# A hybrid decoder layer on one core: direct terms of 19 blocks a feed-forward added by a transfer, with six smaller edits

## The chip, the core and the metric

The kernel runs on one core of a Trainium2 chip. Its engines work side by side, each through its own queue of instructions in order: TensorE (PE; its weight loads are PEld) multiplies matrices into PSUM banks, VectorE (DVE) and ScalarE (ACT) do elementwise work, GpSimd (POOL) here mostly issues transfers, SyncE (SP) issues the loads of weights. Sixteen DMA engines carry the transfers of all queues. The metric is the device time of one execution in microseconds (us); the median of the runs counts.

## The reference

One layer over 256 tokens with a model width of 2048, all in float32:

```python
h = layer_norm(DN_ALPHA * h + 0.5 * swiglu(h, ffn1_w_in, ffn1_w_out), ln1_g, ln1_b)
q, k, v, qi, ki, wi, rx, rg, gates = split_cols(h @ w_in)
...                      # rotary embedding of q, k, qi, ki
y_attn = dsa_attention(q, k, v, qi, ki, wi)
y_rnn = rglru_branch(rx, rg, conv_w, conv_b, lru_wa, lru_ba, lru_wx, lru_bx, lru_lambda)
g_attn, g_rnn = jnp.split(jax.nn.sigmoid(gates), 2, axis=-1)
merged = g_attn * (y_attn @ w_attn_branch) + g_rnn * (y_rnn @ w_rnn_branch)
h = layer_norm(DN_ALPHA * h + merged @ w_out, ln2_g, ln2_b)
h = layer_norm(DN_ALPHA * h + 0.5 * swiglu(h, ffn2_w_in, ffn2_w_out), ln3_g, ln3_b)
```

`swiglu` is `(silu(a) * b) @ w_out` with `a, b = split(h @ w_in)`; its inner width is 5632. The attention has 16 heads of 128; an indexer picks for each query its 64 best keys, the others are masked before the softmax. Weights come to some 460 MB, each read once.

## The kernel before, in words

**Precision by splitting.** Every float32 operand is split in a high and a low part in the format fp32r. ScalarE copies the high part (`wh`, line 243), VectorE subtracts it to get the low part (`wl`, line 244). A product is then three matmuls: high by high, low of the data by high of the weights, high of the data by low of the weights (lines 694, 695, 697). So each weight element costs one ScalarE and one VectorE pass before TensorE can use it.

**Pieces.** The weights are a single list of pieces in order of use, 512 KB each in the plain case (128 partitions by 1024). `Weights.unit` hands out parts of the current piece; when it moves to a new piece it issues loads up to ten pieces ahead (`load_to`, as far as load buffers are free: five plain ones `raw`, three double ones `rf`), emits the split of the piece four ahead (`split_to`), and then steps the background once (`on_piece`). So "n pieces behind" in this text counts such steps.

**Forms.** A chunk is four of the sixteen row tiles of a weight block. A plain chunk (`c`) is two pieces. A chunk in forms replaces eight half-size products with seven, at the price of sums on VectorE: `p1q3`, `p2`, `q5p7`, `q4p6` (function `operand`, lines 206, 210, 213), which multiply sums of weights with sums of the data (`sf`, `sh`, `sl`, function `left`). `block_plan` sets which chunks of a block are plain, which are in forms, and where pieces of an output product (`o`, a fill) stand between them.

**The feed-forwards.** Both run `ffn`: 22 blocks of 256 columns for a and as many for b. `layer_plans` gives the plans: blocks 0 and 1 plain; block 2 chunks 1 and 3 in forms and two fills; blocks 3 to 5 two or three chunks in forms and two fills; blocks 6 to 21 three chunks in forms and four fills, three of them at the head of the block. At the end of a block `gate` adds the forms' results (in banks `e`) and the direct terms (in banks `c`) into a buffer `z` (there is one), takes the silu and the product on ScalarE and VectorE, and some steps later transposes the result on TensorE and splits it to `g`. The transposes stand `LAG_T` = 7 steps behind. `fill` multiplies a segment's `g` with output weights; the segments are blocks 0 to 1, 2 to 5, 6 to 9 and so on. Its results go by ScalarE into `yd` and by an accumulating transfer of POOL's queue into `Y` (lines 1109, 1110).

**Order.** TensorE's, SP's and POOL's instructions stand in the order in which the program emits them. ScalarE's and VectorE's are put in order by a planner from its own estimates and priorities; `tc.high_priority()` moves instructions up, and `tc.issue_after(x)` keeps those inside behind `x`.

**Other places that the change touches.** The start (line 567 on) splits x and the first weight pieces alternately; a copy of one element into the buffer of the third part of x (line 571) makes its load, and all that follow it on SP's queue, wait for the first split. `head` is a step-by-step task for one attention head; its softmax scales and masks the scores in one VectorE instruction (line 1279) and finds the two row maxima in two more (line 1284). `OuterNorm.finish` does the last norm: for the second half of the tokens, blocks 0 and 1 of the output go through TensorE with a diagonal matrix (`by_pe`), 2 and 3 through VectorE alone.

## Time and profile before

| what | us |
|---|---|
| median of 3 runs | 2238.52 (2238.44 to 2239.13) |
| the profiled execution's own time | 2239.67 |
| its span, first to last instruction | 2237.9 |
| TensorE busy in the span | 2223.3 |
| VectorE busy | 2106.7 |
| ScalarE busy | 1429.8 |
| POOL busy | 125.0 |

The span is what the trace shows of the profiled execution; its own time lies 1.8 us above it. An engine's busy time counts instructions that do work and leaves waits out; matmuls are pipelined, so their durations overlap and a row's duration is longer than the distance to the next row. In a row of the order of time the columns are start, length, engine, line, operation, tiles written and read, shape and count; brackets hold the idle time before it and what ended it. The DMA engines are busy for 57.9% of the span with SP's queue and for 8.4% with POOL's.

### The profile page before, as it was taken

The page shows a single profiled execution, that of the slowest core. Times are in us where ns is not written, and L with a number is a line of the kernel's source. Part 1 is how long each engine was busy: PE and PEld are TensorE (multiplying, and loading weights), DVE is VectorE, ACT ScalarE, POOL GpSimd, SP SyncE. Part 2 cuts the span into 40 slices and gives each one's busy share as a digit, 9 for nine tenths or more (in the row PEclk, how much of TensorE's full clock was granted, in tenths as well). Part 3 has the DMA queues.
Part 4 walks back from the last instruction along what each step waited for, and adds up shares of the span by engine and source line. Part 5 has one row for each costly group of instructions (what it writes and reads, how often), then busy time and mean ns, then how long its engine had stood idle before and what let it go on. Part 6 is the DMA issues. An engine that isn't in the chain of part 4 may idle for free. (4 is left out here: it accounts for less than half of the span.)

```text
span 2237.9 us, 38642 instructions
## 1 busy us (share of the span) xinstructions
PE 2223.3 (99%) x14582; PEld 2056.6 (92%) x14582; DVE 2106.7 (94%) x3037; ACT 1429.8 (64%) x1995; POOL 125.0 (6%) x195
## 2 busy tenths in 40 slices
PE   9999999999999999999999999999999999999998
PEld 7999999999998898899999999998889999999997
DVE  8999999999999999899868879999999999999997
ACT  7666666666656655665567786555666666666663
POOL 0000000000001000001000002100000000000001
PEclk9999999999999999999999999999999999999999
DMA  9776666666675555648666668766677667676655
GB/s 328 240 227 232 233 214 226 236 222 236 225 241 194 187 198 177 210 132 302 199 192 194 197 189 324 266 214 205 229 228 230 237 220 239 223 243 215 219 200 188
DMA packets 126186, 498.61 MB, mean 223 GB/s; under 512 B 14608, under 2 KB 17424, under 8 KB 107312
## 3 DMA queue, kind: packets, MB, share of 16 engines
q1 hardware_dynamic: 107424, 451.98, 57.9%
q0 software_dynamic: 18576, 44.17, 8.4%
q8 instruction: 114, 1.87, 0.3%
q14 instruction: 72, 0.59, 0.1%
HBM read 464.63 MB, written 10.49 MB: 212 GB/s over the span
## 5 line engine op out<-in xcount | busy, mean ns | idle before, releaser
L243 ACT ACTIVATE wh<-raw 128x1024 fp32r<-128x1024 f32 (+1 forms) x569 | 575.0, 1028 | 288.6 <-PE mm L695 164.4
L244 DVE TENSOR_TENSOR wl<-raw,wh 128x1024 fp32r<-128x1024 f32 (+1 forms) x569 | 661.9, 1183 | 79.8 <-ACT wh L243 78.6
L243 ACT ACTIVATE wh<-rf 128x1024 fp32r<-128x1024 f32 (+1 forms) x438 | 393.5, 915 | 191.6 <-PE mm L695 103.6
L244 DVE TENSOR_TENSOR wl<-rf,wh 128x1024 fp32r<-128x1024 f32 (+1 forms) x438 | 450.9, 1042 | 7.2 <-ACT wh L243 1.5
L694 PE MATMUL mm<-wh,hs 128*128 128x512 f32 (+1 forms) x872 | 297.3, 350 | 0.0
L695 PE MATMUL mm<-wh,hs 128*128 128x512 f32 (+1 forms) x872 | 292.1, 344 | 0.0
L694 PE MATMUL mm<-wh,g 128*128 128x512 f32 x656 | 249.5, 380 | 1.9 <-DVE z L1076 1.9
L695 PE MATMUL mm<-wh,g 128*128 128x512 f32 x656 | 248.8, 379 | 0.5 <-DVE g L810 0.5
L243 ACT ACTIVATE wh<-ws 128x1024 fp32r<-128x1024 f32 x146 | 155.2, 1063 | 123.9 <-PE mm L695 71.7
L694 PE MATMUL bp<-wh,sh 128*128 128x256 f32 x876 | 213.6, 278 | 0.0
L695 PE MATMUL bp<-wh,sl 128*128 128x256 f32 x876 | 210.7, 275 | 0.0
L697 PE MATMUL mm<-wl,hs 128*128 128x512 f32 (+1 forms) x872 | 205.0, 344 | 0.0
L206 DVE TENSOR_TENSOR ws<-rf 128x1024 f32<-128x1024 f32 x146 | 178.3, 1221 | 8.8 <-DMA rf<-wab 2.8
L244 DVE TENSOR_TENSOR wl<-ws,wh 128x1024 fp32r<-128x1024 f32 x146 | 178.1, 1220 | 2.8 <-ACT wh L243 2.6
L694 PEld LDWEIGHTS mm<-wh,hs 128*128 128x128 f32 x872 | 165.8, 190 | 15.3 <-issue 1.3
L695 PEld LDWEIGHTS mm<-wh,hs 128*128 128x128 f32 x872 | 165.9, 190 | 13.6
L1404 PE MATMUL mm<-hs,wh 128*128 128x256 f32 x640 | 176.4, 276 | 0.0
L1405 PE MATMUL mm<-hs,wh 128*128 128x256 f32 x640 | 176.0, 275 | 0.0
L1406 PE MATMUL mm<-hs,wl 128*128 128x256 f32 x640 | 176.0, 275 | 0.0
L695 PEld LDWEIGHTS bp<-wh,sl 128*128 128x128 f32 x876 | 168.1, 192 | 1.2
L694 PEld LDWEIGHTS bp<-wh,sh 128*128 128x128 f32 x876 | 168.0, 192 | 1.2
L697 PE MATMUL mm<-wl,g 128*128 128x512 f32 x656 | 168.3, 379 | 0.0
(374 smaller groups left out, 4886.5 us busy)
## 6 DMA issues: line engine op xcount, KB each, us to landing
rf<-f1a SPq DMA_DIRECT2D x57, 1024.0 KB, 6.2
rf<-f2a SPq DMA_DIRECT2D x57, 1024.0 KB, 6.0
raw<-f1o SPq DMA_DIRECT2D x88, 512.0 KB, 7.8
raw<-f2o SPq DMA_DIRECT2D x88, 512.0 KB, 7.8
raw<-wB SPq DMA_DIRECT2D x80, 512.0 KB, 4.5
raw<-f2a SPq DMA_DIRECT2D x62, 512.0 KB, 3.9
raw<-f1a SPq DMA_DIRECT2D x61, 512.0 KB, 3.9
raw<-wG SPq DMA_DIRECT2D x54, 512.0 KB, 4.2
```

Source lines behind the costliest of these rows:

```text
L206: v.tensor_tensor(t, b[:, 0:4:3], b[:, 1:2].to_broadcast([P, 2, 4, P]), op=OP.add)
L243: nc.scalar.activation(hp, src, AF.Copy)
L244: self.last = nc.vector.tensor_tensor(lp, src, hp, op=OP.subtract)
L694: T.matmul(ps, xh, w[0], start=start, stop=False)
L695: T.matmul(ps, xl, w[0], start=False, stop=False)
L697: T.matmul(ps, xh, w[1], start=False, stop=stop)
L1404: T.matmul(ps, w[0], xh, start=first, stop=False)
L1405: T.matmul(ps, w[0], xl, start=False, stop=False)
L1406: T.matmul(ps, w[1], xh, start=False, stop=last)
```

## The change

In blocks 2 to 20 of each feed-forward, the direct terms in the banks `c` are no longer added by VectorE. ScalarE copies both banks into a new buffer `u` (4 KB a partition, one of it), and POOL's queue issues an accumulating transfer from `u` to `z`. The silu stands eight steps behind the block's end, after the high part of the piece split last; the product one step after that, behind the last low part; the transposes at the eleventh step. There are six `t` buffers instead of eight and 20 `sm` buffers instead of 21.

The plans are made for each layer. The first keeps two chunks in forms in block 2; the second has only chunk 1 there. In both, block 5 has three chunks in forms where it had two. The weights' layout follows.

At the start the loads of x and of the first four pieces are issued without the wait, and the one-element copy goes. In the softmax, two fused instructions take scores plus mask, times the negative scale, and a running minimum, in place of three; the exponential gets a scale of -1. In the last norm, block 0's first step of the second token half goes ahead of block 2's.

```diff
@@ -51,7 +51,7 @@
 
 U_BUFS = 53
 Z_BUFS = 1
-T_BUFS = 8
+T_BUFS = 6
 RAW_BUFS = 5
 RAWF_BUFS = 3
 WS_BUFS = 1
@@ -93,15 +93,16 @@
     return plan
 
 
-def layer_plans():
+def layer_plans(third=(1, 3)):
     plans = [block_plan((), 0)] * 2
-    plans += [block_plan((1, 3), 2, 0)] + [block_plan(THREE if n == 4 else (1, 3), 2, 0) for n in (3, 4, 5)]
+    plans += [block_plan(third, 2, 0)] + [block_plan(THREE if n > 3 else (1, 3), 2, 0) for n in (3, 4, 5)]
     plans += [block_plan(THREE, 4, 3)] * (NBK - 6)
     return plans
 
 
 FILLS = [(g, nb, 2 * p) for g, (b0, b1) in enumerate(SEGS[:-1]) for nb in range(4) for p in range(b1 - b0)]
 PLANS = layer_plans()
+PLANS2 = layer_plans((1,))
 A_ORDER = (6, 7, None, 4, 5, 0, 1, 2, 3)
 A_FAST = {b: () if b == 6 else ONE_A if b in (5, 1) else FAST_A for b in range(8)}
 GATE_FAST = ((), (), (), (3,), FAST_A, FAST_A, (), ())
@@ -112,12 +113,14 @@
 YR_FORMS = (0, 1)
 MG_FORMS = (0, 1)
 LAG_MG = (7, 3)
-assert sum(f == "o" for p in PLANS for f, _ in p) == len(FILLS)
+assert all(sum(f == "o" for p in q for f, _ in p) == len(FILLS) for q in (PLANS, PLANS2))
 
 OUT_LAST = ([(nb, k) for nb in (0, 1) for k in (0, 2, 4)] + [(nb, 6) for nb in (0, 1)]
             + [(nb, k) for nb in (2, 3) for k in (0, 2, 4, 6)])
 
 LAG_T = (7, 6)
+LAG_Z = 8
+LAG_D = 11
 LAG_LN = 4
 WIDE = (4, 3, 2)
 WARM = 10
@@ -240,7 +243,7 @@
             else:
                 parts = [tuple(x[:, q:min(n, q + step)] for x in (self.raw[k], h, l)) for q in range(0, n, step)]
             for src, hp, lp in parts:
-                nc.scalar.activation(hp, src, AF.Copy)
+                self.last_h = nc.scalar.activation(hp, src, AF.Copy)
                 self.last = nc.vector.tensor_tensor(lp, src, hp, op=OP.subtract)
             self.hl[self.split] = (h, l)
             if form in (None, FORMS[-1]):
@@ -454,7 +457,9 @@
         return r
 
     xs = []
-    W.load_to(1, load_x_fm)
+    W.load_to(3, load_x_fm)
+    for k2 in range(4, NK // 2):
+        load_x_fm(k2)
     cols = C([P, NCOLS], "cols")
     G.dma_start(cols, cols_d)
     posi = C([P, 2], "posi", I32)
@@ -567,11 +572,6 @@
     with tc.manual_schedule():
         for k2 in range(4):
             xs += split_x(k2)
-            if k2 == 0:
-                V.tensor_copy(xraw[2][:, :1], xs[0][:, 1, :1])
-                W.load_to(3, load_x_fm)
-                for j in range(4, NK // 2):
-                    load_x_fm(j)
             W.split_to(k2, (256, 512, PIECE, PIECE)[k2])
         for k2 in range(4, NK // 2):
             xs += split_x(k2)
@@ -967,8 +967,8 @@
                 T.matmul(ps, diag, y, start=False, stop=True)
                 A.activation(y, ps, AF.Copy)
 
+            first(1, 0)
             first(1, 2)
-            first(1, 0)
             by_pe(0)
             second(1, 2)
             leave(1, 0)
@@ -1058,8 +1058,8 @@
                 for t in range(2):
                     done(nb, ps, t)
 
-    def ffn(x, forms, ln):
-        def gate(c, e, g, i, lag, plain):
+    def ffn(x, forms, ln, plans):
+        def gate(c, e, g, i, lag, plain, by_dma):
 
             z = W.fast_pool.tile([P, 4 * S], F32, name=name("z"), tag="z", bufs=Z_BUFS)
             z4 = z.rearrange("p (j c) -> p j c", j=4)
@@ -1070,16 +1070,31 @@
                 V.tensor_tensor(z4[:, 1], z4[:, 0], p6, op=OP.add)
                 V.tensor_tensor(z4[:, 2], z4[:, 1], p7, op=OP.add)
                 V.tensor_tensor(b, q5[:, None, :].to_broadcast([P, 2, S]), z4[:, 1:3], op=OP.subtract)
-                for t in range(2):
-                    w = 512 if plain or t == 0 else S
-                    zt = z[:, t * 512:t * 512 + w]
-                    V.tensor_tensor(zt, zt, c[t][:, :w], op=OP.add)
-                A.activation(a, a, AF.Silu)
+                if by_dma:
+                    u = temps.tile([P, 4 * S], F32, name=name("cc"), tag="cc", bufs=1)
+                    for t in range(2):
+                        A.activation(u[:, t * 512:(t + 1) * 512], c[t], AF.Copy)
+                    G.dma_start(z, u, accum_op=OP.add)
+                    for _ in range(LAG_Z):
+                        yield
+                    with tc.issue_after(W.last_h.ins):
+                        A.activation(a, a, AF.Silu)
+                    yield
+                    with tc.issue_after(W.last.ins):
+                        V.tensor_tensor(a, a, b, op=OP.mult)
+                    lag = LAG_D - LAG_Z - 1
+                else:
+                    for t in range(2):
+                        w = 512 if plain or t == 0 else S
+                        zt = z[:, t * 512:t * 512 + w]
+                        V.tensor_tensor(zt, zt, c[t][:, :w], op=OP.add)
+                    A.activation(a, a, AF.Silu)
             else:
                 for t in range(2):
                     A.activation(z4[:, 2 * t], c[t][:, :S], AF.Silu)
                     A.activation(z4[:, 2 * t + 1], c[t][:, S:], AF.Copy)
-            V.tensor_tensor(a, a, b, op=OP.mult)
+            if not by_dma:
+                V.tensor_tensor(a, a, b, op=OP.mult)
             for _ in range(lag):
                 yield
             ps = BP()
@@ -1113,8 +1128,8 @@
             for n in range(b0, b1):
                 if 2 < n < 6:
                     MM(), MM()
-                c, e = blockF(x, forms, PLANS[n], fill)
-                task = gate(c, e, g[s], 2 * (n - b0), LAG_T[n == NBK - 1], ("c", 0) in PLANS[n])
+                c, e = blockF(x, forms, plans[n], fill)
+                task = gate(c, e, g[s], 2 * (n - b0), LAG_T[n == NBK - 1], ("c", 0) in PLANS[n], 1 < n < NBK - 1 and ("c", 0) in PLANS[n])
                 with tc.high_priority():
                     next(task)
                 bg.add("gate", task)
@@ -1276,15 +1291,16 @@
         T.matmul(ps[:, P:3 * P], q[:, P:], k, start=True, stop=True)
         yield
         s = U("s")[:, :3 * P]
-        V.scalar_tensor_tensor(s, ps[:, :3 * P], ATT_SCALE, bias, op0=OP.mult, op1=OP.add)
         nm = SM(2)
         sm = SM(2)
         part = (s[:, :P], s[:, P:])
         for t in range(2):
-            V.tensor_reduce(nm[:, t:t + 1], part[t], axis=AX, op=OP.max, negate=True)
+            a, b = t * P, (1 + 2 * t) * P
+            V.tensor_tensor_reduce(s[:, a:b], ps[:, a:b], bias[:, a:b], -ATT_SCALE, -2 * NEG, OP.add, OP.min,
+                                   nm[:, t:t + 1])
         yield
         for t in range(2):
-            A.activation(part[t], part[t], AF.Exp, bias=nm[:, t:t + 1], accum_out=sm[:, t:t + 1])
+            A.activation(part[t], part[t], AF.Exp, scale=-1.0, bias=nm[:, t:t + 1], accum_out=sm[:, t:t + 1])
         yield
         V.reciprocal(sm, sm)
         for t in range(2):
@@ -1528,7 +1544,7 @@
     mg = mg_forms = None
 
 
-    ffn(ln.hs, ln.forms, OuterNorm(ln3_g, ln3_b))
+    ffn(ln.hs, ln.forms, OuterNorm(ln3_g, ln3_b), PLANS2)
 
 
 def _layout(x, positions, ffn1_w_in, ffn1_w_out, ln1_g, ln1_b, w_in, conv_w, conv_b, lru_wa, lru_ba,
@@ -1550,8 +1566,8 @@
                 out[b][:, q * 2048:(q + 1) * 2048] = u.transpose(0, 5, 1, 2, 3, 4).reshape(P, -1)
         return out
 
-    def f_in(w):
-        fast = [sorted({k for f, k in plan if f in FORMS}) for plan in PLANS]
+    def f_in(w, plans):
+        fast = [sorted({k for f, k in plan if f in FORMS}) for plan in plans]
         return paired(w.reshape(NK, P, 2, NBK, 256).transpose(3, 1, 0, 2, 4).reshape(NBK, P, NK, 512), fast)
 
     def f_out(w):
```

More of the change, by code (lines that the diff above doesn't have):

```diff
@@ L343, in SM @@
     def SM(n, s="s", dt=F32):
-        return pool.tile([P, 32], dt, name=name(s), tag="sm", bufs=21)[:, :n]
+        return pool.tile([P, 32], dt, name=name(s), tag="sm", bufs=20)[:, :n]
     def C(shape, s, dt=F32):
@@ L376, in block_pieces, with ffn_pieces @@
                 pieces.append((chunk[k], f))
-    def ffn_pieces(fa, fo):
+    def ffn_pieces(fa, fo, plans):
         fills = iter(FILLS)
-        for n, plan in enumerate(PLANS):
+        for n, plan in enumerate(plans):
             block_pieces(fa[n], plan, fills, fo)
@@ L389, in wide @@
         wides.update(range(len(pieces) - n, len(pieces)))
-    ffn_pieces(f1a, f1o)
+    ffn_pieces(f1a, f1o, PLANS)
     wide(WIDE[0])
@@ L420, in tile_layer @@
     wide(WIDE[1])
-    ffn_pieces(f2a, f2o)
+    ffn_pieces(f2a, f2o, PLANS2)
     wide(WIDE[2])
@@ L1133, in tile_layer @@
     ln = InnerNorm("ln1_g", "ln1_b", FAST_A, lambda: bg.add("y", put_away()))
-    ffn(xs, xf, ln)
+    ffn(xs, xf, ln, PLANS)
     hs = ln.hs
@@ L1603, in _layout @@
         pos=c(positions[0].reshape(2, P).T),
-        f1a=f_in(ffn1_w_in[0]), f1o=f_out(ffn1_w_out[0]), wA=a_blocks(w[:, :4096], [A_FAST[b] for b in range(8)]),
+        f1a=f_in(ffn1_w_in[0], PLANS), f1o=f_out(ffn1_w_out[0]), wA=a_blocks(w[:, :4096], [A_FAST[b] for b in range(8)]),
         wki=c(ki.reshape(NK, P, P).transpose(1, 0, 2)).reshape(P, 2048), wB=b_blocks(w[:, 4176:9296].reshape(D, 2, RNN)[:, :, order].reshape(D, -1)),
@@ L1608, in _layout @@
         wrb=a_blocks(w_rnn_branch[0][order], YR_FAST),
-        wo=a_blocks(w_out[0], MG_FAST + ((),)), f2a=f_in(ffn2_w_in[0]), f2o=f_out(ffn2_w_out[0]), cols_d=c(cols),
+        wo=a_blocks(w_out[0], MG_FAST + ((),)), f2a=f_in(ffn2_w_in[0], PLANS2), f2o=f_out(ffn2_w_out[0]), cols_d=c(cols),
         ln1_g=c(ln1_g[0]), ln1_b=c(ln1_b[0]), ln2_g=c(ln2_g[0]), ln2_b=c(ln2_b[0]),
```

## The prediction

> **What bounds the kernel now.** I read the page first, then busy time by stretches of the span, then the order of time on TensorE around the few places where it stands still.
>
> ```profile
> span 2237.9 us, 38642 instructions
> PE 2223.3 (99%) x14582; PEld 2056.6 (92%) x14582; DVE 2106.7 (94%) x3037; ACT 1429.8 (64%) x1995; POOL 125.0 (6%) x195
> ```
>
> TensorE is busy for 2223.3 of 2237.9 us, so at most some 15 us of the span are not its own work. VectorE, which the change mainly relieves, is second at 94%. Busy time by stretches (columns: length, then PE, PEld, DVE, ACT, POOL, then granted clock, DMA share, GB/s):
>
> ```profile
> 0.00:6.00 6.00, 4.08 (x11) 3.27 (x12) 2.38 (x7) 2.96 (x7) 2.26 (x24) 1.00 0.63 187
> 6.00:20.00 14.00, 11.60 (x52) 9.22 (x51) 9.99 (x22) 9.67 (x22) 0.00 (x0) 1.00 1.01 374
> ...
> 1585.00:1640.00 55.00, 52.60 (x301) 46.93 (x300) 53.14 (x78) 30.21 (x42) 1.80 (x2) 1.00 0.75 247
> ...
> 1735.00:2195.00 460.00, 460.00 (x3076) 429.89 (x3075) 455.40 (x535) 299.49 (x366) 26.27 (x30) 1.00 0.67 226
> 2195.00:2238.00 43.00, 36.97 (x190) 31.17 (x188) 31.44 (x51) 12.55 (x19) 6.83 (x7) 1.00 0.46 160
> ...
> 840.00:1010.00 170.00, 169.27 (x988) 151.54 (x987) 154.47 (x343) 106.47 (x189) 5.42 (x10) 1.00 0.55 177
> ```
>
> From 1735 to 2195, fifteen like blocks of the second feed-forward, TensorE has no idle time (460.00 of 460.00), although VectorE is full too (455.40). The attention stretch is alike (169.27 of 170.00). What can be won by unloading VectorE lies only in 6 to 20 (2.4 us idle), 1585 to 1640 (2.4 us idle) and the tail (6 us). A steady block, on TensorE:
>
> ```profile
> 1735.00 0.38 PE L694 MATMUL mm<-wh,g 128*128 128x512 f32 x1
> 1742.77 0.38 PE L694 MATMUL mm<-wh,hs 128*128 128x512 f32 x1
> ...
> 1745.36 0.27 PE L694 MATMUL bp<-wh,hs 128*128 128x256 f32 x1
> ...
> 1746.70 0.28 PE L694 MATMUL mm<-wh,hs 128*128 128x256 f32 x1
> ...
> 1747.37 0.60 PE L1088 MATMUL bp<-ident,z 128*128 128x128 f32 x4
> 1747.72 0.36 PE L694 MATMUL bp<-wh,sh 128*128 128x256 f32 x1
> ...
> 1777.41 0.60 PE L1088 MATMUL bp<-ident,z 128*128 128x128 f32 x4
> ```
>
> From 1735.00 to 1742.77 three pieces of an output fill run: 7.77/3 = 2.59 us a plain piece. From 1745.36 to 1746.70 is one form of 1024 columns (1.34 us), from there to 1747.37 the half-size form p2 (0.67 us); then the four transposes of the block before hold TensorE 0.35 us. The next block's transposes come at 1777.41: a period of 30.04 us, in which TensorE never waits.
>
> **The change part by part.** Profiled time is 2239.67 us, 1.8 above its span and 1.15 above the median of 2238.52; I sum differences and set them on the median.
>
> *The transfer.* In each of 19 blocks a layer VectorE's two additions of the direct terms go, and ScalarE copies both banks out instead. The rows of the block before and of the nearest copy and transfer:
>
> ```profile
> 1739.67 0.68 DVE L1072 TENSOR_TENSOR z<-bp,z 128x512 f32<-128x512 f32 x1
> 1740.39 1.28 DVE L1076 TENSOR_TENSOR z<-z,mm 128x512 f32<-128x512 f32 x2
> ...
> 1749.29 0.42 DVE L810 TENSOR_TENSOR g<-bp,g 128x256 fp32r<-128x256 f32 x1
> ...
> 1751.36 0.42 DVE L810 TENSOR_TENSOR g<-bp,g 128x256 fp32r<-128x256 f32 x1
> ...
> 1741.77 0.64 ACT L1077 ACTIVATE z<-z 128x512 f32<-128x512 f32 x1 [1.19 <-DVE z L1076]
> ```
>
> ```profile
> L1110 POOL DMA_DIRECT2D y<-yd x2: 862/912/961, 1761.6 to 1762.4; - x2
> ...
> DMA to landing us min/median/max: 3.3/4.7/6.1
> ```
>
> ```profile
> L206 DVE TENSOR_TENSOR ws<-rf 128x1024 f32<-128x1024 f32 x146 | 178.3, 1221 | 8.8 <-DMA rf<-wab 2.8 <-DMA rf<-f2a 2.5 <-DMA rf<-wG 1.4
> ...
> L210 DVE TENSOR_TENSOR rf<-ws,rf 128x512 f32<-128x512 f32 x146 | 100.1, 685 | 0.1
> ...
> L1109 ACT ACTIVATE yd<-mm 128x512 f32<-128x512 f32 x80 | 42.6, 584 | 0.0
> ```
>
> VectorE loses 1.28 us a block, 49 us over 38 blocks; ScalarE gains two copies of 0.58 us, 44 us over all, at 64% load. In steady blocks TensorE has no idle time to give back, so this is worth 0 there. Cover: TensorE's own 30.04 us; without it VectorE's 1.28 us a block would show. The new transfer has three hurdles. It cannot start before VectorE's last write to z, 1739.67 + 0.68 = 1740.35. The nearest row is the pair of accumulating 256 KB transfers, the same 512 KB in all: first issue at 1761.6, last landing 6.1 us after the second issue at 1762.4, so 6.9 us. That gives landing at 1747.25. The function now stands at the eighth piece, after ScalarE's split of the piece four ahead: the eighth piece begins after o, o, o, c, p1q3, p2 and q5p7, at 1747.37 + 1.34 = 1748.71. So the transfer is 1.5 us early, and nothing behind the function on ScalarE's queue (the splits of the pieces to come) is held. The transposes move from the seventh piece to the eleventh, 1748.71 + 1.34 + 2.59 + 1.34 = 1753.98. Function (0.64), one split between (about 1.06 on ScalarE by the row at 18.21 below, 1.22 on VectorE) and product (0.69, the size of one addition) take 3.6 us from 1748.71, so they end near 1752.3, 1.7 us ahead of the transposes. Cost 0. On POOL's queue nothing waits behind the new issue until the output transfers of 1761.6. The weight loads on SP's queue share the DMA engines, which are at 0.67; 15 x 512 KB is 7.9 MB on the 104 MB (226 GB/s x 460 us) of those fifteen blocks. The last landing that does no harm is 1753.98 - 3.6 = 1750.4, 10.0 us after the issue (a rival below).
>
> What is late next? Where a segment of four blocks ends (blocks 6, 10, 14, 18 of a layer) the fill at the fourteenth piece uses what the transposes at the eleventh deliver. Now VectorE's second half ends at 1751.36 + 0.42 = 1751.78, 4.41 us after the transposes start. Afterwards the fill needs that half after 0.35 + 0.67 + 2 x 1.34 + 0.86 (its first four matmuls, a third of 2.59) = 4.56 us. It fits by 0.15 us, so I take 0; if one more split of 1.22 us stands ahead, 1.07 us at each of 8 places, +8.6. The lower end is 0, TensorE has no wait there to lose.
>
> *The chunk.* The first layer gets one more chunk in forms (block 5). A plain chunk is two pieces, 5.18 us; in forms it is 3 x 1.34 + 0.67 = 4.69. So -0.5 us. VectorE pays 1.22 (sum), 2 x 0.685 (additions), 3 x 1.22 + 0.69 (splits) = 6.9 against 2.4; blocks 4 and 5 in a row take some 2 x 1.2 us more of VectorE than TensorE gives them, covered by its lead of four pieces and by the 1.28 us a block that went. Ends: -0.5 and +1.9 (that excess unhidden). The second layer moves a chunk from block 2 to block 5: +0.5 and -0.5.
>
> *Start of the second feed-forward.* TensorE and VectorE there:
>
> ```profile
> 1611.64 0.60 PE L1088 MATMUL bp<-ident,z 128*128 128x128 f32 x4
> ...
> 1618.93 0.48 PE L695 MATMUL mm<-wh,g 128*128 128x512 f32 x1 [0.53 <-DVE g L810]
> ...
> 1637.31 0.45 PE L694 MATMUL mm<-wh,g 128*128 128x512 f32 x1 [1.87 <-DVE z L1076]
> ...
> 1618.45 0.42 DVE L810 TENSOR_TENSOR g<-bp,g 128x256 fp32r<-128x256 f32 x1
> ```
>
> TensorE waits 0.53 us for g and 1.87 us for a bank that VectorE's late addition holds. The second goes: ScalarE empties the bank, and VectorE is 4.5 us less loaded by the chunk. But with one chunk in forms the plan of block 2 has 12 pieces, and its second fill, which reads block 1's g, moves from the eleventh piece to the seventh, which is where block 1's transposes (lag seven, unchanged) are issued. So TensorE issues the transposes and needs their product at once. Before, the first half of g came at 1618.45 + 0.42, 7.2 us after the transposes at 1611.64: that is the upper end, 6.8 us after taking off their own 0.35. In the steady block it came at 1749.71, 2.3 us after, so 2.0. The lower end is the operations alone: 0.60 for the transposes, some 0.39 and 0.42 for ScalarE and VectorE, 1.1 us of wait. These steps have high priority here and VectorE's backlog is smaller, so I take 1.5, near the steady row. Net: -0.53 - 1.87 + 1.5 = -0.9; ends -1.3 and +4.4.
>
> *Loads at the start.*
>
> ```profile
> 9.23 0.48 PE L694 MATMUL mm<-wh,xs 128*128 128x512 f32 x1 [0.62 <-ACT wh L243]
> 13.52 0.48 PE L694 MATMUL mm<-wh,xs 128*128 128x512 f32 x1 [1.43 <-ACT wh L243]
> 19.32 0.48 PE L694 MATMUL mm<-wh,xs 128*128 128x512 f32 x1 [0.35 <-ACT wh L243]
> ...
> 5.39 0.33 SPq L444 DMA_DIRECT2D x<-x_fm  x1
> 18.21 1.06 ACT L243 ACTIVATE wh<-raw 128x1024 fp32r<-128x1024 f32 x1 [0.35 <-DMA raw<-f1a]
> ```
>
> TensorE waits 0.62 + 1.43 + 0.35 = 2.40 us for the first pieces. The third transfer of x was held to 5.39; now all go at once, some 2.3 us earlier, in the same order. But the engines are full from 6 us on (share 1.01), and already 0.63 of the first 6 us, of which nearly 2 pass before anything moves: 3.78 us of some 4. What earlier issues can fill is 0.2 to 0.3 us of engine time, and it is the last wait, on the load that ended at 18.21, that counts. I take -0.3, by that row; ends -2.4 (all waits gone) and +0.8 (the second piece, whose wait is 0.62, shares with the later ones).
>
> *Softmax.* One addition-scale of 551 ns and two reductions (276 and 416 ns) become two fused passes over the same data:
>
> ```profile
> L1279 DVE SCALAR_TENSOR_TENSOR s<-bp,bias x16: 539/551/555, 896.2 to 971.8; 128x384 f32<-128x384 f32 x16
> ...
> L1284 DVE TENSOR_REDUCE s<-s x32: 276/348/416, 897.1 to 974.0; 128x1 f32<-128x128 f32 x16, 128x1 f32<-128x256 f32 x16
> ```
>
> Old 1.24 us a head; new between 0.69 (the reductions alone) and 1.6, so VectorE gets between -9 and +6 us over 16 heads, in a stretch where it is busy 154.47 of 170.00 and TensorE 169.27. Hidden by TensorE: 0, ends 0 and +0.7.
>
> *Last norm.*
>
> ```profile
> 2230.22 0.40 ACT L963 ACTIVATE dg<-ident,s 128x128 f32<-128x128 f32 x1 [0.53 <-DVE s L833]
> 2230.98 2.36 PE L967 MATMUL bp<-y,dg 128*128 128x512 f32 x6 [1.24 <-DVE y L948]
> ...
> 2232.86 0.88 DVE L952 SCALAR_TENSOR_TENSOR y<-y,s,row 128x256 f32<-128x256 f32 x2
> 2232.95 0.82 ACT L968 ACTIVATE y<-bp 128x256 f32<-128x256 f32 x2 [0.24 <-PE bp L967]
> ```
>
> TensorE's first product could start when the diagonal is ready, 2230.62, not 2230.98. But VectorE ends at 2233.74 with the same operations, and ScalarE's last copy waits for another TensorE product behind VectorE's next one. 0; ends -0.36 and 0. Fewer buffers (8 to 6, 21 to 20): no row shows a wait on them, so 0; ends 0 and +0.5.
>
> Sum: -0.5 - 0.9 - 0.3 = -1.7 us, 2236.8.
>
> **The rivals.** *Everything lands well*: all start waits go (-2.4), the fill waits only 1.1 (-1.3), chunk -0.5, last norm -0.36, and the slow restart after a wait (0.48 and 0.45 for 0.38 in the rows) is saved some five times, -0.5: -5.1, 2233.4. For it: these waits stand in the trace; against: the DMA share of 1.01 and g's 7.2 us.
>
> *The fills starve* (slower side): at each of the eight segment ends the product of the transposes comes one split later than now. Price 8.6 - 1.7 = +6.9, 2245.4. It decides once more than 0.15 us is added between transposes and g. For it: VectorE is full, so its order decides; against: it has 1.28 us less a block.
>
> *The transfer is late*: it shares its engines with weight loads at a block's start, and lands later than 10.0 us after its issue instead of at 6.9. From there each further us costs 38 us, since what follows it to the transposes is fixed: at 0.4 us late, 15 - 1.7, 2252. For it: the engines' mean share of 0.67; against: the measured pair of 6.9 ran in the same stretch. [...]
>
> *It does nothing*: the waits only move, 2238.5; part of the no-change case.
>
> **How the numbers follow.** A measurement here tells 0.2%, 4.5 us, from nothing. The forecast and its neighbours (no effect among them) have 0.52: no change. Everything lands well has 0.30, below 2234.0: faster. The fills starve 0.12, the late transfer 0.06: slower 0.18. Range: down to 2232 (that case, and some room for waits set at 0), up to 2243, which takes in the upper ends of the start and of block 2 together (+5) and half of the starving fills. The forecast's own range is 2234 to 2240.
>
> **What would show it.** Right: in a steady block no wait at the transposes, period 30.04 still, VectorE near 95%; z's transfer landing some 7 us after its issue; the wait of 1.87 us gone and one of 1 to 2 us at the seventh piece of block 2; first layer 0.5 us shorter at block 5. Wrong: a period above 30.1, waits of TensorE on VectorE's product of z or on g at the fourteenth piece, ScalarE idle before the function; or the start's waits gone altogether.

## The result and the profile after

The changed kernel takes **2263.93 us** (median of 4 runs, 2262.80 to 2265.56), the kernel before in the same comparison 2238.82 (4 runs, 2238.44 to 2239.55): a ratio of 1.0112 with a 95% interval of 1.0099 to 1.0124, 25.1 us slower. The forecast was 2236.8, a small gain, with a range of 2232.0 to 2243.0.

The page after, its first lines and its queue of software-made transfers (packets, MB, share of the engines):

```profile
span 2262.4 us, 38763 instructions
PE 2233.2 (99%) x14600; PEld 2061.0 (91%) x14600; DVE 2067.9 (91%) x2981; ACT 1468.5 (65%) x2073; POOL 157.5 (7%) x233
...
q0 software_dynamic: 24048, 64.09, 12.8%
```

VectorE is relieved as planned: 38.8 us less busy than before, 91% in place of 94%. ScalarE has 38.7 us more, for its copies. The span is 24.5 us longer all the same. Stretches of the same lengths as before (length, then PE, PEld, DVE, ACT, POOL, clock, DMA share, GB/s):

```profile
1585.00:1640.00 55.00, 49.45 (x239) 43.02 (x239) 48.52 (x81) 29.10 (x41) 3.40 (x5) 0.94 0.71 226
...
1735.00:2195.00 460.00, 458.22 (x3073) 426.81 (x3073) 436.46 (x500) 312.83 (x396) 39.17 (x45) 1.00 0.76 243
```

In the steady stretch VectorE is at 95%, as forecast, but TensorE, which had no idle time before, now has some; and at the start of the second feed-forward it is idle 5.6 us of 55 and its clock is granted at 0.94 only. What TensorE and its weight loads wait for (total, times, longest):

```profile
PE bp L1103 <- issue: 6.7, 3, 2.7
PE mm L695 <- DVE g L810: 5.1, 1, 5.1
...
PE mm L694 <- ACT wh L246: 1.0, 2, 0.7
...
PEld bp L1103 <- PE mm L697: 9.0, 32, 0.3
```

Line 1103 is the four transposes of a block. The list has three groups: 32 short waits at the transposes, a few long ones there, and a single one of 5.1 us for g. They are taken one by one.

**Steady blocks (5 to 20 of each layer).** One of them in order of time, with the rows that matter of VectorE, ScalarE, POOL and TensorE (the row at 1768.43 is TensorE's first of the eighth piece):

```profile
1761.03 0.86 POOL L1077 DMA_DIRECT2D z<-cc  x1 [8.03 <-ACT wh L246]
...
1768.23 1.06 ACT L246 ACTIVATE wh<-ws 128x1024 fp32r<-128x1024 f32 x1 [0.43 <-ACT wh L246]
1768.43 0.28 PE L694 MATMUL mm<-wh,hs 128*128 128x256 f32 x1
...
1769.19 0.61 ACT L1081 ACTIVATE z<-z 128x512 f32<-128x512 f32 x1
1769.66 1.22 DVE L247 TENSOR_TENSOR wl<-ws,wh 128x1024 fp32r<-128x1024 f32 x1
1770.91 1.22 DVE L209 TENSOR_TENSOR ws<-rf 128x1024 f32<-128x1024 f32 x1
1772.06 1.22 DVE L247 TENSOR_TENSOR wl<-rf,wh 128x1024 fp32r<-128x1024 f32 x1
1773.19 0.68 DVE L1084 TENSOR_TENSOR z<-z 128x512 f32<-128x512 f32 x1
...
1773.98 0.63 PE L1103 MATMUL bp<-ident,z 128*128 128x128 f32 x4
...
1804.33 0.63 PE L1103 MATMUL bp<-ident,z 128*128 128x128 f32 x4
```

The function (line 1081) does not wait for its transfer, which had landed at 1767.82, 6.8 us after the issue and 1.4 us ahead of it. But its product (line 1084) starts 3.39 us after the function's end. VectorE's queue holds three operations of 1.22 us each in between: a low part, a sum and another low part. The product ends at 1773.87, 0.11 us ahead of the transposes, and these are 0.28 us late (9.0 us over 32). The list of waits names the matmul before the transposes, which ends at about the same time as the product; experiment 9 tells the two apart. The period is 1804.33 - 1773.98 = 30.35 us in place of 30.04. The landing has no part in it: in the block whose transfer is issued at 1912.81 it takes 9.3 us, the function waits 0.80 us for it, and the transposes are 0.28 us late as in the others.

**Blocks 2 to 4.** The first layer, the same lines for blocks 2 and 3, and the summary of all 38 transfers:

```profile
81.60 0.85 POOL L1077 DMA_DIRECT2D z<-cc  x1 [8.38 <-ACT wh L246]
91.11 0.63 ACT L1081 ACTIVATE z<-z 128x512 f32<-128x512 f32 x1 [2.42 <-DMA z<-cc]
93.86 0.69 DVE L1084 TENSOR_TENSOR z<-z 128x512 f32<-128x512 f32 x1
94.65 0.69 PE L1103 MATMUL bp<-ident,z 128*128 128x128 f32 x4 [2.02 <-issue]
...
110.46 0.85 POOL L1077 DMA_DIRECT2D z<-cc  x1 [7.89 <-PE bp L695]
119.82 0.63 ACT L1081 ACTIVATE z<-z 128x512 f32<-128x512 f32 x1 [3.09 <-DMA z<-cc]
122.57 0.68 DVE L1084 TENSOR_TENSOR z<-z 128x512 f32<-128x512 f32 x1
123.36 0.63 PE L1103 MATMUL bp<-ident,z 128*128 128x128 f32 x4 [2.73 <-issue]
```

```profile
DMA to landing us min/median/max: 5.5/6.7/9.5
```

Here the function does wait for the transfer, which lands 9.5 and 9.3 us after its issue. From the function's start to the product's end another 3.4 us pass, and 2.1 of them are again the product's place in VectorE's queue (from the function's end at 91.74 to 93.86). TensorE wanted the transposes at 94.65 - 2.02 = 92.63, 11.0 us after the issue, and in block 3 at 120.63, 10.2 us after it. In the steady block that distance is 1773.98 - 0.28 - 1761.03 = 12.7 us. The same eleven pieces are a shorter time there, because these blocks have fewer fills. In block 4 the transfer lands 6.1 us after its issue at 139.16, so that lateness is not the same in all three; there the function hardly waits (0.52 us), the product starts 2.4 us behind it, and the transposes wait 0.70 us. The second layer has 0.37, 1.95 and 0.70 us in its blocks 2 to 4; the six waits make 8.5 us.

**Second feed-forward, block 2.** VectorE between the transposes of block 1 and the fill at the seventh piece:

```profile
1624.39 0.60 PE L1103 MATMUL bp<-ident,z 128*128 128x128 f32 x4
...
1626.01 2.35 DVE L247 TENSOR_TENSOR wl<-raw,wh 128x1024 fp32r<-128x1024 f32 x2
1628.28 1.22 DVE L209 TENSOR_TENSOR ws<-rf 128x1024 f32<-128x1024 f32 x1
1629.42 1.22 DVE L247 TENSOR_TENSOR wl<-rf,wh 128x1024 fp32r<-128x1024 f32 x1
1630.55 0.42 DVE L810 TENSOR_TENSOR g<-bp,g 128x256 fp32r<-128x256 f32 x1
...
1631.02 0.79 PE L695 MATMUL mm<-wh,g 128*128 128x512 f32 x1 [5.08 <-DVE g L810]
```

The transposes' product lies ready at 1625, and VectorE gets to g's low part at 1630.55, behind residual additions and four weight operations. TensorE stands for 5.08 us. What follows is slow too (same columns as the stretches above):

```profile
94.60:99.00 4.40, 4.35 (x15) 3.60 (x16) 3.16 (x4) 0.65 (x2) 0.00 (x0) 0.61 0.40 106
1625.40:1631.00 5.60, 0.48 (x1) 0.19 (x1) 5.60 (x7) 0.01 (x1) 0.00 (x0) 0.70 0.69 236
1631.00:1635.40 4.40, 4.38 (x13) 3.62 (x14) 0.90 (x2) 1.32 (x2) 0.00 (x0) 0.60 0.83 300
```

After this wait, and after the 2.02 us in block 2, TensorE's granted clock is 0.6 on average over 4.4 us; the last section looks at it more closely.

### The profile page after: what moved, and what is told of

The parts are those of the page before. It is cut to its first block, busy times and chain, and to the rows that moved or that the text cites. A ratio compares the mean times of both kernels' runs of the same rounds, so it can differ in the third digit from the quotient of the medians.

```text
span 2262.4 us, 38763 instructions
## 1 busy us (share of the span) xinstructions
PE 2233.2 (99%) x14600; PEld 2061.0 (91%) x14600; DVE 2067.9 (91%) x2981; ACT 1468.5 (65%) x2073; POOL 157.5 (7%) x233
## 3 DMA queue, kind: packets, MB, share of 16 engines
q8 instruction: 114, 1.87, 0.3%
## 5 line engine op out<-in xcount | busy, mean ns | idle before, releaser
L247 DVE TENSOR_TENSOR wl<-raw,wh 128x1024 fp32r<-128x1024 f32 (+2 forms) x567 | 662.6, 1185 | 123.5 <-ACT wh L246 121.3
L246 ACT ACTIVATE wh<-raw 128x1024 fp32r<-128x1024 f32 (+2 forms) x567 | 575.8, 1028 | 278.2 <-PE mm L695 163.7
L246 ACT ACTIVATE wh<-rf 128x1024 fp32r<-128x1024 f32 (+1 forms) x441 | 398.8, 915 | 216.8 <-PE mm L695 137.1
L247 DVE TENSOR_TENSOR wl<-rf,wh 128x1024 fp32r<-128x1024 f32 (+1 forms) x441 | 456.9, 1043 | 22.3 <-ACT wh L246 21.0
```

The lines of the kernel that those rows point to most:

```text
L246: self.last_h = nc.scalar.activation(hp, src, AF.Copy)
L247: self.last = nc.vector.tensor_tensor(lp, src, hp, op=OP.subtract)
```

## The experiments

Each edit is against the changed kernel unless said otherwise; each time stands beside the kernel before on the same chip (2238.28 for the first four, 2238.37 for the next four, 2239.45 for the last four), and the interval of each ratio is 0.0009 to 0.0017 to either side, 2 to 4 us. "Back" counts how much of the 25.1 us a run does not have, each run and the change against the kernel before on its own chip.

**1. The plans of before in the second layer.** Takes the fill off the seventh piece.

```diff
-PLANS2 = layer_plans((1,))
+PLANS2 = layer_plans()
```

> The changed kernel, but block 2 of the second feed-forward keeps two chunks in forms as in the first. Theory (three separate waits: the fill at the seventh piece of block 2; the transfer's late landing in blocks 2 to 4; the product of silu behind one more sum on VectorE in blocks 5 to 20): the 5.1 us wait at that fill goes, with some 2 us at a lower clock behind it, and at most 2 us of other waits come back: 2257 to 2259. Rival (VectorE is simply late there, whatever the plan): the wait moves to the next piece that needs g, less than 2 us are won: 2262 to 2264.

2261.31 us, 1.0101 [1.0086, 1.0116]: only 2 us back. The wait at the fill is gone, but now the transfer of block 2 of that layer is late:

```profile
1644.74 0.85 POOL L1077 DMA_DIRECT2D z<-cc  x1 [10.00 <-DVE z L1072]
1655.23 0.63 ACT L1081 ACTIVATE z<-z 128x512 f32<-128x512 f32 x1 [5.44 <-DMA z<-cc]
1658.77 1.09 PE L1103 MATMUL bp<-ident,z 128*128 128x128 f32 x4 [5.03 <-DVE z L1084]
```

The transfer, held until VectorE's last write to z, lands 10.5 us after its issue, and TensorE wants the transposes 9.0 us after it; in the changed kernel these were 7.0 and 15.6 us. So this plan takes one wait away and makes another of the same length, and the run doesn't tell what the fill alone is worth; experiment 10 does.

**2. No transfer at all**, the two additions back on VectorE, all else as changed.

```diff
-..., 1 < n < NBK - 1 and ("c", 0) in PLANS[n])
+..., False)
```

> The changed kernel, with VectorE adding the direct terms of all blocks as before (transposes seven pieces behind); plans, loads, softmax, last norm and buffers stay changed. Theory: the waits at the transposes go altogether, some 20 us of the 25: 2242 to 2246, with the wait at the fill of block 2 still there. Rival (the smaller edits or the fewer buffers cost as much): 2250 or more.

2247.05 us, 1.0040 [1.0025, 1.0055]. The transfer with its lags carries 16.3 of the 25.1 us; 8.8 remain without it. What TensorE waits for then:

```profile
PE mm L695 <- DVE g L810: 3.8, 1, 3.8
...
PE bp L1103 <- DVE z L1097: 1.8, 2, 0.9
```

The wait at the seventh piece stays, a little shorter, and the extra chunk in block 5 makes the transposes of the block before late, once in each layer, with 0.9 us more for two banks that VectorE holds there. These waits are absent from the changed kernel, where the additions are off VectorE.

**3. The function one piece earlier.**

```diff
-LAG_Z = 8
+LAG_Z = 7
```

> The changed kernel with function and product one piece earlier (seven behind), transposes still at the eleventh. Theory for blocks 5 to 20: the product stands behind one more sum of VectorE than it should, so 32 waits of 0.28 us at the transposes go, 9 us: 2254 to 2257; blocks 2 to 4 stay as they are. Rival (the transfer's landing decides in these blocks too): the function waits on ScalarE for the transfer, nothing is won: 2263 or more.

2260.66 us, 1.0102 [1.0085, 1.0119]. The short waits in the steady blocks go, but:

```profile
PE mm L695 <- DVE g L810: 7.2, 7, 3.8
PE bp L1103 <- issue: 5.0, 3, 1.7
PE bp L1103 <- DVE z L1084: 3.9, 1, 3.9
```

Besides the 3.8 us at the seventh piece, six fills now wait for g, 3.4 us together, and ScalarE waits for a transfer 17 times, 27.4 us in all, where it was 5 times and 9.1. An earlier function sets ScalarE's weight splits behind the transfer, so this is no cure.

**4. The transfer from block 6 on.**

```diff
-..., 1 < n < NBK - 1 and ("c", 0) in PLANS[n])
+..., 5 < n < NBK - 1 and ("c", 0) in PLANS[n])
```

> The changed kernel with the transfer in blocks 6 to 20 alone; blocks 2 to 5 as before. Theory (late landing is a matter of the short blocks 2 to 4, whose eleventh piece comes sooner and whose loads are denser): some 11 us go, 2251 to 2254. Rival (the first blocks that use the transfer wait, whichever they are): the waits of 2 to 3 us appear in blocks 6 to 8: 2258 or more.

2256.20 us, 1.0080 [1.0065, 1.0095]. The long waits of blocks 2 to 4 are gone, the 0.28 us of the steady blocks are not (8.4 us over the 30 blocks left with a transfer). Against experiment 2 on the same chip, which has most of the other waits of this run but not these, this is 9.2 us more. The two waits of 0.9 us at the transposes and the 0.9 us for two banks are here too, since VectorE has the additions of blocks 2 to 5 again.

**5. The transfer alone**, put into the kernel before (with its buffers), every other edit left out; the lines added are those of the diff under `if by_dma`.

```diff
-T_BUFS = 8
+T_BUFS = 6
+LAG_Z = 8
+LAG_D = 11
+                if by_dma: ...
```

> The kernel before with the transfer alone (lags eight and eleven, blocks 2 to 20 of both layers, and the fewer buffers that make room); plans, loads, softmax and last norm as before. Theory (the transfer's waits are the loss): the steady waits (32 x 0.28 = 9 us), late landings in blocks 2 to 4 of the first layer (6 to 8) and of the second (6 to 8 with two chunks in forms in block 2): 2259 to 2264. Rival (the other edits take part in the loss, through the plans above all): under 2255.

2270.21 us, 1.0135 [1.0120, 1.0151]: 31.8 us slower, more than with the other edits and more than either theory had.

```profile
PE bp L1106 <- DVE z L1087: 12.3, 3, 4.7
```

With the plans of before, blocks 2 and 3 are both short in both layers. Their four waits make 14.0 us (12.3 and one of 1.7), with landings up to 10.6 us after the issue; the steady waits make 9.7. Each of the three longest waits is followed by 5.3 to 5.8 us at half clock, which costs an estimated 8.4 us more, half of their sum (last section). Together that is 32.1 for the 31.8.

**6. The small edits alone** in the kernel before: loads at once, softmax in one pass, last norm.

```diff
-    W.load_to(1, load_x_fm)
+    W.load_to(3, load_x_fm)
+    for k2 in range(4, NK // 2):
+        load_x_fm(k2)
...
+            V.tensor_tensor_reduce(s[:, a:b], ps[:, a:b], bias[:, a:b], -ATT_SCALE, -2 * NEG, OP.add, OP.min, ...)
...
-            first(1, 2)
             first(1, 0)
+            first(1, 2)
```

> The kernel before with loads at once, softmax in one pass and the last norm's order, nothing else. Theory (from the idle time of TensorE by stretches in the runs so far: start -0.7, a wait of 0.9 in the attention that went, tail -0.8): 2235.5 to 2236.5 where before is 2238.3. Rival (these gains are the other edits' or are given back later): 2238 to 2239.

2238.98 us, 1.0002 [0.9993, 1.0011]: nothing that can be measured.

**7. Plans of before, transfer from block 6, all lags one piece shorter**, with the small edits. An attempt at a better version: no short block has a transfer, and function and transposes come a piece sooner.

```diff
-LAG_Z = 8
-LAG_D = 11
+LAG_Z = 7
+LAG_D = 10
```

> The small edits, the plans of before, the transfer in blocks 6 to 20 alone, function seven and transposes ten pieces behind. Theory: with the function one piece earlier the product stands ahead of the sum, and with the transposes one earlier the fills at the fourteenth piece have their g again, so the transfer costs nothing and wins nothing in these blocks: 2235.5 to 2238. Rival (ScalarE now waits for the transfer in front of the function, or g is late still): waits at the transposes or fills of 0.3 us and more a block, 2242 or more.

2244.26 us, 1.0025 [1.0014, 1.0035], 5.9 us slower than the kernel before. With the function at the seventh piece ScalarE waits for landings:

```profile
ACT z L1081 <- DMA z<-cc: 13.8, 16, 2.5
```

In five places of the second layer's steady stretch, and in one of the first's, this reaches the transposes, 4.3 us in all. Seven pieces are too few for the later landings. The bank's wait of the kernel before is still there (1.72 us), and this time 3.4 us at half clock follow it, some 1.7 us more.

**8. Two pieces more in blocks 2 to 4**, so that the steady block's distance in time is about met.

```diff
-                    for _ in range(LAG_Z):
+                    for _ in range(LAG_Z + extra):        # extra = 2 * (1 < n < 5)
```

> The changed kernel, with function, product and transposes of blocks 2 to 4 two pieces later than in the other blocks. Theory (in the short blocks eight pieces are less time than the transfer takes): the waits at the transposes of blocks 2 to 4 in both layers go, with the low clock behind them, 8 to 11 us: 2253 to 2256. Rival (VectorE's order, not the landing, holds the product there): they stay, 2261 or more.

2256.73 us, 1.0081 [1.0067, 1.0094]: 6.7 us back. Waits of 2.0 and 2.7 us at the transposes of blocks 2 and 3 of the first layer became 0 and 0.5, but block 4's went from 0.7 to 1.2 us; there the function waits for nothing, and the product starts 4.1 us behind it. ScalarE waits for a transfer twice, 1.6 us in all.

**9. The product in the function's step** rather than one step later.

```diff
-                    yield
                     with tc.issue_after(W.last.ins):
                         V.tensor_tensor(a, a, b, op=OP.mult)
-                    lag = LAG_D - LAG_Z - 1
+                    lag = LAG_D - LAG_Z
```

> The changed kernel with the product in the same step as the function (both eight pieces behind); function, transfer and transposes stay where they are. Theory (in blocks 5 to 20 VectorE's queue holds the product behind a sum and a low part that it does not need): the 32 waits of 0.28 us go, and in blocks 2 to 4 the product follows the function at once instead of 2.1 us later, which takes most of the 9.4 us waited there: 2244 to 2250. Rival (the landing decides even in the steady blocks): 2260 or more.

2249.23 us, 1.0044 [1.0030, 1.0058]: 15.3 us of the 25.1 back by one line moved. The steady block now:

```profile
1757.42 0.63 ACT L1081 ACTIVATE z<-z 128x512 f32<-128x512 f32 x1
1759.02 0.69 DVE L1083 TENSOR_TENSOR z<-z 128x512 f32<-128x512 f32 x1
...
1761.91 0.60 PE L1102 MATMUL bp<-ident,z 128*128 128x128 f32 x4
...
1791.96 0.60 PE L1102 MATMUL bp<-ident,z 128*128 128x128 f32 x4
```

The product starts 0.97 us behind the function in place of 3.39, ends 2.2 us ahead of the transposes, and the period is 30.05 us again. The transfer is unchanged and lands 5.5 to 8.5 us after its issue in these blocks (5.6 to 9.3 in the changed kernel), so in steady blocks the loss was the product's place in VectorE's queue. In blocks 2 and 3 of the first layer the transfer still lands late, 8.6 and 9.2 us after its issue, but with the product right behind the function the waits at the transposes fall from 2.02 and 2.73 us to 0 and 0.51. So there too the late landing alone was not enough. Over blocks 2 to 4 of both layers 3.8 us of the 8.5 are left.

**10. Block 1 of the second layer three pieces sooner**, so that its transposes no longer meet the fill.

```diff
-..., LAG_T[n == NBK - 1], ...
+..., 4 if n == 1 and ln.last else LAG_T[n == NBK - 1], ...
```

> The changed kernel with block 1 of the second layer transposed four pieces behind instead of seven. Theory (the fill at the seventh piece of block 2 waits because the transposes are issued in the same step): the wait of 5.1 us and the low clock behind it go: 2256 to 2259. Rival (VectorE is simply behind there, as keeping two chunks in forms suggested, which won 2.6): the wait moves to the transposes of blocks 2 and 3: 2261 or more.

2255.67 us, 1.0072 [1.0058, 1.0086]: 8.9 us back against the kernel before on each chip (25.1 to 16.2). The wait for g is gone from the list; the waits at the transposes of blocks 2 to 4 stay, 7.3 us in place of 8.5.

**11. Experiments 8, 9 and 10 together.**

> The three together: product in the function's step, blocks 2 to 4 two pieces later, block 1 of the second layer four pieces behind. Theory (these three waits are the whole loss): 2238 to 2242. Rival (a part of the loss is elsewhere, in ScalarE's copies or the loads that share the engines): 2246 or more.

2237.84 us (11 runs, 2237.62 to 2240.81), 0.9994 [0.9985, 1.0003]. The whole loss is gone.

```profile
1615.00:1660.00 45.00, 45.00 (x278) 41.26 (x277) 42.14 (x50) 31.47 (x41) 5.25 (x6) 1.00 0.83 258
1735.00:2195.00 460.00, 460.00 (x3073) 429.41 (x3072) 437.44 (x504) 313.60 (x394) 39.25 (x45) 1.00 0.75 243
```

TensorE is full again in both stretches, at full clock, with VectorE at 95% in the steady one. (The block transposed sooner by experiment 10 waits 1.05 us, at 1607.92.) It is no faster than the kernel before by anything that can be measured.

**12. The bank early, without a transfer**: in the kernel before, with the loads, the softmax and the fewer buffers of the change, ScalarE copies the banks out in block 2 of the second layer only, and VectorE adds the copies.

```diff
+                if early:                                  # ln.last and n == 2
+                    u = temps.tile([P, 4 * S], F32, name=name("cc"), tag="cc", bufs=1)
+                    for t in range(2):
+                        A.activation(u[:, t * 512:(t + 1) * 512], c[t], AF.Copy)
```

> The kernel before with loads at once and softmax in one pass, and in block 2 of the second feed-forward alone ScalarE copies the banks out while VectorE still adds the copies; six t buffers. Theory (the wait of 1.87 us there is for the bank alone): it goes, 2235 to 2237. Rival (VectorE's lateness shows at the next piece instead): 2238 to 2239.

2239.02 us, 0.9999 [0.9990, 1.0008]. The 1.87 us for the bank are gone, and two other waits stand in the list:

```profile
PE bp L859 <- DVE y L878: 1.5, 1, 1.5
PE bp L1090 <- DVE z L1084: 0.8, 1, 0.8
```

The wait of 0.8 us, at 1639.02, is at the next transposes, whose data VectorE has late: freeing the bank lets TensorE run to the next thing that VectorE owes. The one of 1.5 us, at 1554.83, lies ahead of the edit; why it is longer than before (0.4) is not shown. The time shows no gain, -0.4 us, but its interval of -2.2 to +1.8 would just hold one of 1.87.

Against what was expected: the times of experiments 1 to 5 lie in none of the ranges; those of 8, 10 and 11 miss the theory's range by less than 1 us; 9 lies in the theory's, 6 and 7 in the rival's, and 12 at the edge of the rival's.

**The sum.** Two ways to add up the 25.1 us. By runs: experiment 9 gives 15.3 back and experiment 10 gives 8.9, 24.2 together. Experiment 8's 6.7 can't be added, since 8 and 9 both shorten the waits of blocks 2 and 3; no run has 9 and 10 without 8. By the changed kernel's own trace: 9.0 us of steady waits, 8.5 in blocks 2 to 4, 5.6 for the two halves of g, and an estimated 3.4 for half clock behind two of these waits (twice 1.7, last section) make 26.5; the kernel before has 2.4 us of waits at the start of the second feed-forward that are gone. That leaves 24.1 for a span that is 24.5 longer, with smaller waits left out. The runs' differences are good to some 4 us each, so that they close this well is partly luck; that experiment 11 closes the loss in one run isn't.

## Why the prediction was wrong

**Unloading VectorE earns nothing in steady blocks: right.** Experiments 9 and 11 have the period back at 30.05 us with VectorE 16 to 18 us less busy in 460, and no time is won.

**The transfer, cost 0: wrong, the largest error (9.0 us in steady blocks).** The step that failed is "Function (0.64), one split between [...] and product (0.69 [...]) take 3.6 us from 1748.71". It has two faults. The count of what stands between: one split, 1.06 and 1.22 us, puts the product 2.28 us behind the function's end; the trace has 3.39, because the product is queued one step later, behind all that VectorE does in that step, three operations of 1.22 us, one of them a sum for a later form. That is 1.1 us more. And the start: the eighth piece begins at 1768.43, but the function at 1769.19, behind ScalarE's split of the same step, 0.8 us that were left out. Together 1.8 us against the 1.7 us in hand; with the 0.1 us from the product's end to the transposes the wait is the measured 0.28. Experiment 9 mends the first fault alone and the wait is gone. Landing (6.8 us for 6.9) and its distance to the function (1.4 us for 1.5) were as reckoned.

**The same working for all 19 blocks: wrong (8.5 us of waits in blocks 2 to 4 of both layers).** The prediction worked out one steady block and multiplied. In blocks 2 and 3 of the first layer both sides of the margin differ: TensorE comes to the transposes 11.0 and 10.2 us after the issue instead of 12.7, and the landing takes 9.5 and 9.3 us instead of 6.8. The product's place adds 2.1 us to both; experiment 9 takes that away and 0.5 us of 4.75 is left, experiment 8 gives more time instead and 0.5 is left as well. In block 4 the landing is not late and the product's place is what the rows show. The rival of the late transfer was right on the late landing in blocks 2 and 3 (that sharing with the weight loads is its cause was the author's estimate and is not shown), but put the point at which it decides at 10.0 us after the issue, the steady block's; with the product's real place it is some 7.5 and 6.7 us there (11.0 and 10.2 less 3.4 and 0.1). That rival was also priced at every block or none. The kernel before already had a sign of it: its output transfers of 256 KB between 90 and 155 us landed 4.9 to 12.1 us after their issue, median 8.2, where the prediction took its 6.9 from the steady stretch. The steady transfers landed 5.6 to 9.3 us after their issue, and none of the 38 took longer than 9.5.

**The seventh piece, 1.5 us with bounds 1.1 to 6.8: the mechanism was right, the size off.** Measured 5.08 us of wait, 0.47 before it for ScalarE's half, and a slow clock behind it. The step that failed is the choice between the bounds: "VectorE's backlog is smaller" was argued from one chunk less, while the residual additions stay in this very stretch, and g's row of before from there (its end 7.2 us after the transposes' start) was the nearest row. Measured, g's low part ended 1630.97 - 1624.39 = 6.6 us after them. Even the upper end left out the clock: from 1631.02 to 1635.20 twelve matmuls of 512 columns take 4.2 us for the 2.6 that a plain piece took at full clock (2.59 in the kernel before), 1.6 us more.

**The bank's 1.87 us: gone, as forecast**, but experiment 12 finds no gain by it alone, and 0.8 us of it shows up again at the next transposes. Its interval leaves open what it is worth.

**The chunk, -0.5: right where VectorE is relieved.** In experiment 11 the first layer takes 150.68 - 58.47 = 92.21 us from the fill ahead of block 1's transposes to block 6's first, in the kernel before 152.21 - 59.47 = 92.74: 0.5 us less, too little to see in the time. Experiment 2 shows two waits of 0.9 us at the transposes when VectorE keeps the additions, against an upper end of 1.9 us that was reckoned for one layer. In experiment 11, with the additions off VectorE, they are gone (its 1.1 us at a block's transposes is block 1's in the second layer, made three pieces sooner).

**Start, softmax, last norm: small, as forecast.** At the start the waits for ScalarE's splits went from 2.4 us in three to 1.0 in two, more than the 0.3 taken; yet experiment 6, which has the three edits together, shows no gain, 0.6 us with an interval of -1.6 to 2.5.

**The fills at the fourteenth piece, a margin of 0.15 us: held** in the changed kernel, which has a single wait for g, the one at the seventh piece. The margin is thin: in experiment 11 two fills wait 0.3 us each, in experiment 3, with the function a piece earlier, six wait, 3.4 us in all. The rival of the starving fills was right in kind and did not decide.

Without the three faults the forecast sum of -1.7 agrees with experiment 11 (-0.06%, -0.15 to +0.03%, about -1.3 us), though that can't be told from no change. What the prediction lacked was hardly the price of an operation but a count of what stands in front of it.

## What to carry to other kernels

When an operation is put some steps later in a schedule, count all that its engine has queued in those steps, and what the step itself puts first, from a row-by-row stretch of the trace, not one typical instruction, and compare with the margin in hand; here a product that waited only in its engine's queue cost 9.0 us in the steady blocks, where no landing held the transposes. A lag in pieces is a lag in time only where pieces are alike: work out the margin for the shortest block and for the stretch with the latest landings as well as for the steady one. Relieving VectorE, at 94%, won nothing here where TensorE was full (16 to 18 us less busy in 460, the same period), but the transfer that relieved it brought a new chain with its own deadline and cost 16.3 us (experiment 2).

## What the hardware showed

**A wait of TensorE cost more where it filled 1.97 us or more of one stretch of 3.41 us of the granted clock.** The trace records the granted clock. Between the start and the end of the changed kernel it has only two values, 1.00 and 0.50, and it is 0.50 from 95.08 to 98.49 and from 1627.66 to 1634.49 us. All times between two changes are whole multiples of 3.413 us: 1 and 2 for the slow stretches, 448 between them; a length of 3.413 us is called a window here. In the slow stretches matmuls of 512 columns start every 0.43 us instead of every 0.22.

Laid out as windows from these times, the wait of 2.02 us in block 2 (92.63 to 94.65) lies in one window, 91.67 to 95.08, and the next is slow. The longer wait in block 3 (120.63 to 123.36) has a border at 122.39 in it, 1.75 us fall in one window and 0.97 in the next, and no window is slow. The wait for g has 5.08 us, with 0.47 ahead of it; 2.20 us of idle time fall in the window from 1624.25, and the clock is at half from that window's end until 3.5 us after the wait.

The same count over all fourteen profiled executions, from the first recorded full clock to the last window before the end, gives this: all 15 windows at full clock in which TensorE is idle for 1.97 us or more are followed by a slow one; of the others, some 9100, only one is, with 1.72 us, while one with 1.95 us is not. So 1.97 us of idle time in a window of 3.41 were enough here, and a slow window that TensorE fills costs an estimated 1.7 us, half its length, since matmuls start there every 0.43 us instead of 0.22.

**One transfer size, landings from 5.5 to 9.5 us.** The three transfers quoted above, from issue to landing (columns as before, the last GB/s):

```profile
81.60:91.10 9.50, 9.50 (x60) 8.72 (x59) 8.20 (x9) 3.82 (x4) 0.85 (x1) 1.00 0.91 271
110.46:119.80 9.34, 9.34 (x63) 8.70 (x62) 8.68 (x10) 4.15 (x4) 0.85 (x1) 1.00 0.90 253
1761.03:1767.80 6.77, 6.77 (x45) 6.26 (x44) 5.28 (x6) 3.70 (x4) 0.86 (x1) 1.00 0.81 241
```

The transfer is 0.52 MB each time. The share of the DMA engines is 0.91 and 0.90 in the late ones and 0.81 in the steady one, which suggests that other loads make it land later. But block 4's transfer (139.16 to 145.23) landed after 6.1 us at a share of 1.06, with 307 GB/s moving, so the load at the time doesn't decide alone. No run changed the loads, and the cause of the late landings stays open. What the rows do show is that one landing time, taken from a pair of transfers in a steady stretch, does not hold for other blocks.
